# Ranking a recorded program's operations by the dependent chain behind them

## The chip, the cores and the metric

The kernel runs on one core of a Trainium2 chip. The metric is device time in microseconds of one launch, the median of several runs; lower is better. The core has TensorE (PE in the profile, with its weight loads as PEld), VectorE (DVE), ScalarE (ACT), GpSimd (POOL, unused here) and SyncE (SP), which issues the DMAs. Each engine works off its own instructions in the order in which the program holds them, and waits at an instruction until what it needs has been signalled.

## The reference

Two request groups, `p` with 1024 tokens and `s` with 512, go through the same two layers. In each layer

```python
hn = rmsnorm(h, norm_g[l])
z = hn @ w_in[l]                                  # 1024 -> 3328 columns
o_hg  = hgrn2_branch(...)     # gated linear recurrence, chunks of 64, both directions
o_lru = rglru_branch(...)     # width-4 convolution, two gates, linear scan, both directions
o_da  = diff_attn_branch(...) # difference of two softmaxes, 4 heads, partial rotary
o = jnp.concatenate([o_hg, o_lru, o_da], axis=-1)
h = h + o @ w_out[l]
gate = jax.nn.sigmoid(h @ ple_gate_w[l])
h = h + gate * (p[l] @ ple_w[l])
```

and a last rmsnorm follows. Everything is float32.

## The kernel before

**Tiles.** Activations lie transposed, 128 features by 512 tokens. A product with a weight is done in three passes on operands that are split into a rounded part and a remainder: weight hi times x hi, weight lo times x hi, weight hi times x lo. So every weight tile `wr` (128x512) is loaded by a DMA (L351), rounded by ACT into `wh` (L352), and its remainder `wl` is made by DVE (L353). `proj` (L356 on) issues, for each tile of four 128x128 blocks, three groups of four matmuls, one for each pass, all through the helper `mm` (L309), into a PSUM bank named `pj`.

**Stages.** For a layer and a group, stage A (`phase_a`) projects to queries, keys, values, gates and recurrence inputs, writes these to DRAM, and then runs three sessions that read them back: attention `at` (`attn`, scores into `big`, row maximum `nm` L664, exponential `pp` L667, difference L674, transposes L682, product with the values into `ov`), the LRU (`lru`, its own weight tile `gwr` L718, its gate matmuls into `big` L746, tanh and exponentials on ACT L753 to L757, products and scans on DVE L767 to L790) and HGRN2 `hg` (`hg_unit` with six levels of products on DVE and small 64x64 matmuls, then `hg_fin`). Attention and HGRN2 end in `head_tail`: a transpose into `pt` (L490), a norm on DVE, a second transpose (L506), a product with the gate. Stage B (`phase_b`) does the output product, the gate product and the residual, and sums squares for the next norm in `acc` (L1095), which `stats_rs` hands to PE (L376). The order of the stages is A of `p`, A of `s`, B of `p` (two blocks of 512 tokens), B of `s`, twice.

**What sets the order.** The code doesn't issue anything directly. Each call is recorded as an operation (`Recorder.__call__`) with its engine, an estimated occupation `occ` and latency `lat`, and the operations that it depends on. `order` then plays a list scheduler: time after time it takes, over all engines, the ready operation that could begin earliest, and on an engine, among those that could begin at once, the one with the lowest `prio`. Before, the priority is the number of the operation in the recording order plus offsets written by hand: weight tiles 400 earlier (`WOFF`), evictions of projections 900 earlier (`EVAC`), statistics 2000 earlier. Buffers of a role are handed out in recording order. `issue` then emits the instructions in that order, and this is the order in which each engine's queue holds them on the chip.

```python
o.prio = o.seq + self.off + off                   # L85
...
def push(o):
    bisect.insort(ready[o.eng], (o.prio, o.seq))  # L133
```

**Buffers that the steps below speak of.** There are two `big` accumulators (each two PSUM banks), three `pj` banks, four `wr` tiles shared by all weight loads, `gwr` among them, and two `ev` tiles for evictions on their way to DRAM.

Of the kernel before, what the change touches and what calls it, by code (L numbers as in the profile page):

```python
# [13 lines left out]
AF = mybir.ActivationFunctionType  # L14
# [18 lines left out]
        "m2x": 9, "m4x": 9, "m2y": 8, "m4y": 6}  # L33
WOFF, EVAC = 400, 900
BANKS = {"pj": 3, "pt": 2, "ov": 1}
LANE = {
# [6 lines left out]
class T:  # L43


    __slots__ = ("tag", "shape", "dt", "name", "t", "uses", "end", "role", "cls", "first")
# [12 lines left out]
class Op:  # L59
    __slots__ = ("eng", "occ", "lat", "fn", "deps", "succ", "nd", "rt", "new", "old", "prio", "seq", "fin", "tab", "nbytes", "stage", "c0", "c1")  # L60


class Recorder:
# [54 lines left out]
    def order(self):  # L118
# [3 lines left out]
        for o in ops:  # L122
            for d in o.deps:
                ops[d].succ.append(o.seq)
        free = {e: 0.0 for e in ("PE", "DVE", "ACT", "POOL", "SP")}
        ready = {e: [] for e in free}
# [111 lines left out]
def tile_trunk(ctx: ExitStack, tc: tile.TileContext, a, groups, depth):  # L238
    nc = tc.nc
# [41 lines left out]
    def V(w, fn, r, wr, ps_=0.0, sc=0.0, off=0):  # L281
        occ = 0.07 + w / 960.0 + ps_ + sc if w > 64 else 0.075
        return R("DVE", occ, fn, r, wr, lat=occ + (0.09 if w > 64 else 0.1), off=off)

    def A(w, fn, r, wr, extra=0.0, tab="exp", off=0):
        occ = 0.07 + w / 1200.0 + extra
        return R("ACT", occ, fn, r, wr, lat=occ + 0.11, tab=tab, off=off)

    def PE(occ, fn, r, wr, off=0):
        return R("PE", occ, fn, r, wr, lat=occ + 0.2, off=off)  # L290
# [13 lines left out]

    MM = 0.236
    B2 = 128 * 512 * 4
# [208 lines left out]
    def phase_a(l, g, n, xs, mid):  # L515
# [105 lines left out]
        def attn(hf):  # L621
# [16 lines left out]
            for tb in range(nb):  # L638
# [9 lines left out]
                for qt in range(4):  # L648
                    wts = []
                    for H in range(2):  # L650
                        P = []
                        s2 = small("s2", 1)
                        for j in range(2):
# [4 lines left out]
                            def f(pv=pv, k=k, q=q, qt=qt):  # L658
# [8 lines left out]
                            A(n, lambda p=p, pv=pv, nm=nm, s1=s1, s2=s2, j=j, qt=qt, H=H: nc.scalar.activation(  # L667
                                out=p.t, in_=pv(), func=AF.Exp, bias=nm.t, accum_out=s1[:, qt, H : H + 1] if j == 0 else s2.t), [b, nm], [p, sk], extra=0.28)
                            P.append(p)
# [17 lines left out]
                    for kb in range(nb):  # L687

                        def f(kb=kb, wts=wts, ov=ov, qt=qt):
                            for kt in range(4 * kb, 4 * kb + 4):  # L690
                                for H in range(2):
                                    mm(ov[H * 64 : H * 64 + 64, qt * 128 : qt * 128 + 128], dv[kt // 4][:, kt % 4, H * 64 : H * 64 + 64],
                                       wts[H][:, kt * 128 : kt * 128 + 128], start=kt == 0, stop=kt == n // 128 - 1)

                        PE(0.83, f, [dv[kb], (wts[0], kb), (wts[1], kb)], [ov])
                e2 = small("e2")
# [99 lines left out]
        def hg_unit(hp_, tb, ro, keep):  # L796
# [23 lines left out]
            def scores(kt, rk, rhs):  # L820
# [7 lines left out]

                PE(0.5, f, [kt, rk], [b])
                return b, lambda: b[:, :, 0:256].rearrange("p h (t i) -> p h t i", t=4)  # L830
# [6 lines left out]
            for li, bb in enumerate(LEVELS):  # L837
                yield
                nbk = 512 // bb
                kc = M2("kc")  # L840
                A(512, lambda kc=kc, bb=bb: nc.scalar.copy(kc.t.rearrange("p (x h r) -> p x h r", h=2, r=bb), diag(KP.t, bb)), X(KP), [kc], extra=0.06)  # L841
                b, pv = scores(kc, QP, lambda p, c, bb=bb: diag(QP[p], bb, c * 64, 64))
# [8 lines left out]

                ex = 0.15 if li % 2 == 0 else 0.0
                V(512, lambda bb=bb, tk=tk: nc.vector.tensor_tensor(out=diag(KP.t, bb), in0=diag(KP.t, bb), in1=tk(), op=MUL), [*X(KP), *tkeys], X(KP), sc=ex)  # L853
# [37 lines left out]

            PE(0.8, f, [*X(KT), v], [pi])
            E = M4("E")
# [10 lines left out]

            PE(0.5, f, [v, ST], [po])
            o2 = T("m2y", [128, 2, 4, 64], F32, "o2", ro.get("o2"))
# [349 lines left out]
```

## Time and profile before

| | |
|---|---|
| median of 3 runs | 2166.9 us (2164.67 to 2170.54) |
| the profiled execution: its own time | 2168.66 us |
| the profiled execution: span from first to last instruction | 2166.9 us |
| PE busy | 2033.9 us, 94% of the span |
| DVE busy | 1540.7 us, 71% |
| ACT busy | 1146.5 us, 53% |
| mean granted TensorE clock | 0.966 of full speed |
| DMA | 318.63 MB, mean 147 GB/s |

The page gives busy time as a share of the whole span, then the same in 40 slices, with the clock that the chip granted to TensorE in each slice. A group of instructions is told with its total and mean time, and the idle time of the engine just before it with what ended it. The table by windows gives each engine's busy time in a stretch that one chooses, and the timeline gives the instructions one by one, with what each waited for in brackets. TensorE's clock has two levels, 1.2 and 2.4 GHz; a granted clock of 0.91 over a stretch means that it stood at the lower one for 18% of it.

### The profile page before, as it was taken

How to read it: one execution, taken by the hardware profiler on the slowest of the kernel's cores; microseconds unless marked ns; L12 is line 12 of the kernel's file. 1: busy time of each engine (PE TensorE's matmuls, PEld its weight loads, DVE VectorE, ACT ScalarE, POOL GpSimd, SP SyncE). 2: the span in 40 equal slices, each digit the busy share in tenths (PEclk: the TensorE clock that was granted, in tenths of full speed). 3: DMA queues.
4: the chain of work that ended last, by engine and by line, in shares of the span. 5: the costliest groups of instructions: out<-in, count | busy, mean ns of one | idle time of the engine just before them, and what ended most of it. 6: DMA issues, size and time to landing. Idle time of an engine off the chain costs nothing.

```text
span 2166.9 us, 38237 instructions
## 1 busy us (share of the span) xinstructions
PE 2033.9 (94%) x14584; PEld 1663.2 (77%) x14584; DVE 1540.7 (71%) x2921; ACT 1146.5 (53%) x1957; POOL 0.2 (0%) x4
## 2 busy tenths in 40 slices
PE   7998999999999888999979988999999999989897
PEld 6887887788887676877758876778778878667786
DVE  5425867788898888754462658686999988874654
ACT  4215866667555337643332557666745654853332
POOL 0000000000000000000000000000000000000000
PEclk9999989999999999999989989999999999999998
DMA  4336423355353446565543453232464344646462
GB/s 149 112 110 195 143 97 116 105 159 167 127 159 113 146 155 198 174 217 162 175 156 117 128 170 121 83 120 90 126 203 157 123 155 161 202 148 220 133 217 73
DMA packets 187576, 318.63 MB, mean 147 GB/s; under 512 B 22017, under 2 KB 40961, under 8 KB 187393
## 3 DMA queue, kind: packets, MB, share of 16 engines
q1 hardware_dynamic: 187392, 316.19, 45.4%
q8 instruction: 115, 1.88, 0.4%
q14 instruction: 69, 0.56, 0.1%
HBM read 231.16 MB, written 84.93 MB: 146 GB/s over the span
## 4 chain that ended last, share of the span: by engine, by line
PE 65%; DVE 6%; ACT 5%; DMA 5%; issue 2%; SPq 0%; DVEq 0%; ACTq 0%
PE pj L309 48%; PE big L309 8%; PE ov L309 4%; PE pt L682 3%; PE pt L309 1%; DMA qk_p<-ev 1%; DMA p<-in_p_p 1%; DMA qk_s<-ev 1%; ACT tr L753 1%; DVE wl L353 1%; ACT tr L757 1%; ACT ti L753 1%; DMA cs<-in_c_cos 1%; PE pt L506 1%; ACT L761 0%
## 5 line engine op out<-in xcount | busy, mean ns | idle before, releaser
L309 PE MATMUL pj<-act,wh 128*128 128x512 f32 x3648 | 946.6, 399 | 22.9 <-ACT act L320 13.7
L309 PEld LDWEIGHTS pj<-act,wh 128*128 128x128 f32 x3648 | 684.1, 191 | 174.1 <-ACT act L320 18.0
L309 PE MATMUL pj<-act,wl 128*128 128x512 f32 x1824 | 489.1, 399 | 2.1 <-DVE wl L353 2.1
L353 DVE TENSOR_TENSOR wl<-wr,wh 128x512 fp32r<-128x512 f32 x400 | 271.6, 686 | 204.0 <-PE pj L309 145.2
L352 ACT CAST wh<-wr 128x512 fp32r<-128x512 f32 x400 | 244.3, 620 | 299.7 <-PE pj L309 228.9
L309 PEld LDWEIGHTS pj<-act,wl 128*128 128x128 f32 x1824 | 343.9, 192 | 76.4 <-DVE wl L353 3.0
L667 ACT ACTIVATE pp<-big,nm 128x1024 f32<-128x1024 f32 (+1 forms) x192 | 187.4, 977 | 72.9 <-DVE nm L664 67.0
L664 DVE TENSOR_REDUCE nm<-big 128x1 f32<-128x1024 f32 (+1 forms) x192 | 198.0, 1034 | 14.9 <-PE big L309 14.3
L309 PE MATMUL pj<-wh,act 128*128 128x256 f32 x768 | 148.8, 292 | 2.7 <-DVE ev L321 2.7
L309 PEld LDWEIGHTS pj<-wh,act 128*128 128x128 f32 x768 | 127.0, 197 | 9.8 <-DVE ev L321 3.3
L685 ACT COPY wt<-pt 128x512 f32<-128x512 f32 x160 | 93.0, 587 | 64.0 <-PE pt L682 56.0
L309 PE MATMUL big<-ks,qs 96*128 96x512 f32 x320 | 113.4, 428 | 9.3 <-ACT pp L667 8.5
L309 PE MATMUL pj<-wl,act 128*128 128x256 f32 x384 | 110.8, 288 | 0.9 <-DVE wl L353 0.8
L674 DVE SCALAR_TENSOR_TENSOR pp<-pp,cc 128x1024 f32<-128x1024 f32 (+1 forms) x96 | 105.6, 1100 | 0.8
L682 PE MATMUL pt<-ident,pp 128*128 128x128 f32 x640 | 94.6, 277 | 3.7 <-ACT ev L612 2.8
L682 PEld LDWEIGHTS pt<-ident,pp 128*128 128x128 f32 x640 | 75.5, 141 | 22.0 <-ACT ev L612 3.2
L309 PE MATMUL ov<-wt,dv 128*64 128x128 f32 x1280 | 88.2, 279 | 0.4 <-ACT wt L685 0.4
L309 PEld LDWEIGHTS ov<-wt,dv 128*64 128x64 f32 x1280 | 68.6, 136 | 22.0 <-issue 18.4
L309 PEld LDWEIGHTS pj<-wl,act 128*128 128x128 f32 x384 | 75.3, 196 | 1.5 <-DVE wl L353 1.5
L309 PE MATMUL pj<-act,ph 128*128 128x512 f32 x192 | 62.7, 403 | 14.3 <-ACT act L320 10.6
L309 PEld LDWEIGHTS big<-ks,qs 96*128 96x128 f32 x320 | 55.2, 192 | 22.6 <-ACT pp L667 11.3
L841 ACT COPY kc<-KP 128x512 f32<-128x512 f32 x72 | 48.5, 674 | 42.9 <-DVE KP L853 32.6
(186 smaller groups left out, 2467.7 us busy)
## 6 DMA issues: line engine op xcount, KB each, us to landing
wr<-in_w_in SPq DMA_DIRECT2D x176, 256.0 KB
wr<-in_w_out SPq DMA_DIRECT2D x96, 256.0 KB
wr<-in_w_gate SPq DMA_DIRECT2D x96, 256.0 KB
h_p<-bh SPq DMA_DIRECT2D x48, 256.0 KB
sg_p<-ev SPq DMA_DIRECT2D x32, 256.0 KB
wr<-in_w_v SPq DMA_DIRECT2D x32, 256.0 KB
qk_p<-ev SPq DMA_DIRECT2D x32, 256.0 KB
act<-oT_p SPq DMA_DIRECT2D x32, 256.0 KB
```

Of the source, the lines that this page charges most:

```text
L309: nc.tensor.matmul(out, lhsT, rhs, start=start, stop=stop, skip_group_check=True)
L352: A(w, lambda raw=raw, hi=hi: nc.scalar.copy(hi.t, raw.t), [raw], [hi], off=o)
L353: V(w, lambda raw=raw, hi=hi, lo=lo: nc.vector.tensor_tensor(out=lo.t, in0=raw.t, in1=hi.t.bitcast(F32), op=SUB), [raw, hi], [lo], off=o)
L506: PE(0.436, lambda: [nc.tensor.transpose(pb[:, c], ot[:, c], ident) for c in cols], [ot, "ident"], [pb])
L664: V(n, lambda nm=nm, pv=pv: nc.vector.tensor_reduce(out=nm.t, in_=pv(), axis=mybir.AxisListType.X, op=ALU.max, negate=True), [b], [nm])
L667: A(n, lambda p=p, pv=pv, nm=nm, s1=s1, s2=s2, j=j, qt=qt, H=H: nc.scalar.activation(out=p.t, in_=pv(), func=AF.Exp, bias=nm.t, accum_out= ...
L674: V(n, lambda P=P, c=c: nc.vector.scalar_tensor_tensor(out=P[0].t, in0=P[1].t, scalar=c.t, in1=P[0].t, op0=MUL, op1=ADD), [P[0], P[1], c], ...
L682: nc.tensor.transpose(pt[:, kt * 128 : kt * 128 + 128], P[0][:, c0 : c0 + 128], ident)
L685: A(512, lambda wt=wt, pt=pt, kb=kb: nc.scalar.copy(wt[:, blk(kb)], pt.t), [pt], [(wt, kb)])
L753: A(512, lambda dst=dst, pg=pg, gt=gt, dr=dr, hb=hb, col=col: nc.scalar.activation(out=dst[:, dr, :], in_=pg[:, gt, :], func=AF.Tanh, scal ...
L757: A(512, lambda tr=tr, dr=dr, col=col: nc.scalar.activation(out=tr[:, dr, :], in_=tr[:, dr, :], func=AF.Exp, scale=d["n4"][:, col], bias=d ...
L841: A(512, lambda kc=kc, bb=bb: nc.scalar.copy(kc.t.rearrange("p (x h r) -> p x h r", h=2, r=bb), diag(KP.t, bb)), X(KP), [kc], extra=0.06)
```

## The change

Each operation gets a `rank`: its own estimated latency plus the largest rank among those that depend on it, so the estimated length of the longest dependent chain that starts with it. The rank in microseconds, times `RANK` (1.0), is taken off the priority. The offsets written by hand stay. Beside that, estimated durations are changed: matmuls, the fixed parts of DVE and ACT operations, and single operations of attention and HGRN2. No operation is added, removed or given other operands; what is issued differs in its order alone.

```diff
+RANK = 1.0
...
+        for o in reversed(ops):
+            o.rank = o.lat + max((ops[x].rank for x in o.succ), default=0.0)
+        for o in ops:
+            o.prio -= o.rank * RANK
         free = {e: 0.0 for e in ("PE", "DVE", "ACT", "POOL", "SP")}
...
     def V(w, fn, r, wr, ps_=0.0, sc=0.0, off=0):
         occ = 0.07 + w / 960.0 + ps_ + sc if w > 64 else 0.075
-        return R("DVE", occ, fn, r, wr, lat=occ + (0.09 if w > 64 else 0.1), off=off)
+        return R("DVE", occ, fn, r, wr, lat=occ + (0.06 if w > 64 else 0.08), off=off)
 
     def A(w, fn, r, wr, extra=0.0, tab="exp", off=0):
-        occ = 0.07 + w / 1200.0 + extra
-        return R("ACT", occ, fn, r, wr, lat=occ + 0.11, tab=tab, off=off)
+        occ = 0.085 + w / 1200.0 + extra
+        return R("ACT", occ, fn, r, wr, lat=occ + 0.08, tab=tab, off=off)
...
-    MM = 0.236
+    MM = 0.2305
...
-                                out=p.t, in_=pv(), func=AF.Exp, bias=nm.t, accum_out=s1[:, qt, H : H + 1] if j == 0 else s2.t), [b, nm], [p, sk], extra=0.28)
+                                out=p.t, in_=pv(), func=AF.Exp, bias=nm.t, accum_out=s1[:, qt, H : H + 1] if j == 0 else s2.t), [b, nm], [p, sk], extra=0.18)
...
-                        PE(0.83, f, [dv[kb], (wts[0], kb), (wts[1], kb)], [ov])
+                        PE(0.98, f, [dv[kb], (wts[0], kb), (wts[1], kb)], [ov])
...
-                PE(0.5, f, [kt, rk], [b])
+                PE(0.3, f, [kt, rk], [b])
...
-                ex = 0.15 if li % 2 == 0 else 0.0
+                ex = 0.0
...
-            PE(0.8, f, [*X(KT), v], [pi])
+            PE(0.55, f, [*X(KT), v], [pi])
...
-            PE(0.5, f, [v, ST], [po])
+            PE(0.35, f, [v, ST], [po])
```

One more estimate of the same kind, that of the copy `kc`, goes from 0.06 to 0.2 extra. The new lines push the code down by five lines, so that what is L309 before is L314 after, L506 is L511, and so on.

**PE at the end of layer 0's sessions.** `o` and `ot` are the tiles of `head_tail`, `pj` the projections, `big<-q,kc` the first matmuls of HGRN2 of group `s`. Before:

```order
L309 MATMUL pj<-act,wl 128x512 x4
L309 MATMUL pj<-act,wh 128x512 x4
L309 MATMUL ov<-wt,dv 64x128 x8
L490 MATMUL pt<-ident,o 128x128 x4
L506 MATMUL pt<-ident,ot 128x128 x4
L309 MATMUL pt<-QP,E 64x64 x30
L490 MATMUL pt<-ident,o 128x128 x4
L506 MATMUL pt<-ident,ot 128x128 x8
L309 MATMUL pj<-act,wh 128x512 x8
L309 MATMUL pj<-act,wl 128x512 x8
```

And with the change:

```order
L314 MATMUL pj<-act,wh 128x512 x4
L511 MATMUL pt<-ident,ot 128x128 x4
L314 MATMUL ov<-wt,dv 64x128 x8
L314 MATMUL pj<-act,wh 128x512 x4
L314 MATMUL pj<-act,wl 128x512 x4
L495 MATMUL pt<-ident,o 128x128 x4
L314 MATMUL pj<-act,wh 128x512 x12
L314 MATMUL big<-q,kc 64x64 x16
L314 MATMUL pj<-act,wl 128x512 x4
L314 MATMUL big<-QP,kc 64x64 x16
L314 MATMUL pj<-act,wl 128x512 x4
L314 MATMUL pj<-act,wh 128x512 x4
```

Before, the three last transposes of `ot` follow each other with no projection between them, and only stage B's first projections come behind. Now the last but one of them stands second in the piece, projections of stage A stand between all of them, the last of them comes six rows below the piece, and the first matmuls of the next HGRN2 unit have moved up among the projections.

**SP in stage A of layer 1, group `p`.** `gwr` is the weight tile of the LRU's second quarter, `qk_p` the evicted queries and keys on their way to DRAM, `nh` the next group's input. Before:

```order
L789 DMA sg<-sg_p 128x512
L589 DMA qk_p<-ev 8x16x512
L351 DMA wr<-in_w_in 128x512
L589 DMA qk_p<-ev 8x16x512
L476 DMA nh<-h_s 128x512
L351 DMA wr<-in_w_in 128x512
L476 DMA nh<-h_s 128x512
L589 DMA qk_p<-ev 8x16x512 x2
L476 DMA nh<-h_s 128x512
L589 DMA qk_p<-ev 8x16x512 x2
L718 DMA gwr<-in_lru_w 128x512
```

And with the change:

```order
L794 DMA sg<-sg_p 128x512
L723 DMA gwr<-in_lru_w 128x512
L594 DMA qk_p<-ev 8x16x512
L735 DMA zp<-lx_p 128x514
L594 DMA qk_p<-ev 8x16x512
L796 DMA oT_p<-s 128x512
L481 DMA nh<-h_s 128x512
L356 DMA wr<-in_w_in 128x512 x2
```

The load of `gwr` has moved past six writes of `qk_p`, two weight loads and three loads of `nh`. On PE the four groups of gate matmuls that need it have moved up by 12 groups.

**DVE at the end of stage B of layer 1, group `p`, first block.** `acc` is the sum of squares that PE waits for, `ti` and `T` are LRU tiles of group `s`. Before:

```order
L353 TENSOR_TENSOR wl<-wr,wh 128x512
L770 SCALAR_TENSOR_TENSOR T_20347<-tr,T_20347 128x1024
L771 TENSOR_TENSOR ti<-ti,T_20347 128x1024
L1095 TENSOR_TENSOR acc<-acc,ev 128x512
L1086 SCALAR_TENSOR_TENSOR ev<-ev,pj 128x512
L775 SCALAR_TENSOR_TENSOR ti<-tr,ti 128x512
L1087 SCALAR_TENSOR_TENSOR h_19819<-ev,h_19819 128x512
L783 SCALAR_TENSOR_TENSOR ti<-tr,ti 128x512
L1095 TENSOR_TENSOR acc<-acc,ev 128x512
```

And with the change:

```order
L1092 SCALAR_TENSOR_TENSOR h_19791<-ev,h_19791 128x512
L772 SCALAR_TENSOR_TENSOR ti<-ti,u 128x1024
L330 TENSOR_TENSOR act<-act 128x512
L1100 TENSOR_TENSOR acc<-acc,ev 128x512
L330 TENSOR_TENSOR act<-act 128x512
L336 TENSOR_SCALAR rv<-ov 128x4
L775 SCALAR_TENSOR_TENSOR T_20381<-tr,T_20381 128x1024
L339 TENSOR_SCALAR ry<-rv 128x4
L776 TENSOR_TENSOR ti<-ti,T_20381 128x1024
```

Two products and two scans of the LRU, which stood ahead of the last addition to `acc`, now stand behind it.

## Rows read from the trace of the kernel before

**Rows 1.** The page: span, busy time, and granted clock in 40 slices.

```profile
span 2166.9 us, 38237 instructions
...
PE 2033.9 (94%) x14584; PEld 1663.2 (77%) x14584; DVE 1540.7 (71%) x2921; ACT 1146.5 (53%) x1957; POOL 0.2 (0%) x4
...
PEclk9999989999999999999989989999999999999998
```

**Rows 2.** Windows: stretch, length, PE, PEld, DVE, ACT, POOL busy; PEclk, DMA.

```profile
702.00:756.00 54.00, 45.75 (x582) 35.78 (x580) 45.78 (x108) 21.27 (x36) 0.00 (x0) 0.91 0.43 138
756.00:810.00 54.00, 48.27 (x563) 38.42 (x556) 44.31 (x110) 21.37 (x36) 0.00 (x0) 0.91 0.48 162
1737.00:1791.00 54.00, 54.00 (x616) 42.58 (x614) 45.70 (x108) 25.79 (x48) 0.00 (x0) 1.00 0.48 160
1791.00:1845.00 54.00, 54.00 (x632) 43.69 (x632) 47.91 (x115) 24.11 (x41) 0.00 (x0) 1.00 0.49 162
1242.00:1296.00 54.00, 44.53 (x255) 38.89 (x254) 27.26 (x37) 28.97 (x42) 0.00 (x0) 0.87 0.62 181
1296.00:1350.00 54.00, 45.79 (x248) 37.63 (x246) 46.60 (x63) 40.53 (x61) 0.00 (x0) 0.91 0.41 131
1890.00:1944.00 54.00, 46.00 (x192) 37.11 (x193) 39.43 (x67) 33.07 (x52) 0.00 (x0) 0.91 0.36 119
```

**Rows 3.** Waits of PE: who for whom, us in total, times, longest us.

```profile
PE ov L309 <- DVE acc L1095: 18.7, 4, 7.9
...
PE big L309 <- ACT pp L667: 8.5, 4, 6.7
PE pt L506 <- DVE ot L502: 6.8, 3, 4.3
PE big L309 <- ACT gwh L320: 6.7, 2, 4.0
...
PE big L309 <- DVE ul L321: 5.6, 2, 3.0
...
PE pj L309 <- DVE wl L353: 2.9, 5, 1.4
```

**Rows 4.** Timeline from 702 us: start, length, engine, instruction, idle before it.

```profile
718.35 1.09 PE L506 MATMUL pt<-ident,ot 128*128 128x128 f32 x4 [4.29 <-DVE ot L502]
...
719.09 3.76 PE L309 MATMUL pj<-act,wh 128*128 128x512 f32 x8
```

**Rows 5.** Timeline from 1239 us, stage A of layer 1, group p.

```profile
1239.93 1.98 PE L309 MATMUL pj<-act,wh 128*128 128x512 f32 x8
...
1242.97 0.33 SPq L351 DMA_DIRECT2D wr<-in_w_in  x1
...
1258.76 0.40 SPq L718 DMA_DIRECT2D gwr<-in_lru_w  x1
...
1263.83 0.62 ACT L320 CAST gwh<-gwr 128x512 fp32r<-128x512 f32 x1 [2.45 <-DMA gwr<-in_lru_w]
...
1264.50 0.79 PE L309 MATMUL big<-uh,gwh 128*128 128x512 f32 x1 [3.98 <-ACT gwh L320]
```

**Rows 6.** Timeline from 1326 us, attention of layer 1, group p.

```profile
1333.41 1.20 DVE L664 TENSOR_REDUCE nm<-big 128x1 f32<-128x1024 f32 x1
...
1335.90 1.22 PE L309 MATMUL big<-ks,qs 96*128 96x512 f32 x2 [6.72 <-ACT pp L667]
```

**Rows 7.** Timeline from 1921 us, end of stage B's first block, layer 1.

```profile
1921.55 1.23 DVE L770 SCALAR_TENSOR_TENSOR T<-tr,T 128x1024 f32<-128x1024 f32 x1 [1.83 <-ACT T L761]
...
1928.72 1.87 PE L309 MATMUL ov<-ones,acc 128*128 128x1 f32 x8 [7.92 <-DVE acc L1095]
```

**Rows 8.** Windows of the densest stretch: all engines, then DVE on `wl` alone.

```profile
432.00:702.00 270.00, 268.12 (x2932) 218.15 (x2927) 240.25 (x508) 164.81 (x315) 0.00 (x0) 1.00 0.46 144
...
432.00:702.00 270.00, 36.54 (x54) 1.00 0.46 144
```

More of the change, by code (lines that the diff above doesn't have):

```diff
@@ L59 @@
 class Op:
-    __slots__ = ("eng", "occ", "lat", "fn", "deps", "succ", "nd", "rt", "new", "old", "prio", "seq", "fin", "tab", "nbytes", "stage", "c0", "c1")
+    __slots__ = ("eng", "occ", "lat", "fn", "deps", "succ", "nd", "rt", "new", "old", "prio", "seq", "fin", "tab", "nbytes", "rank", "stage", "c0", "c1")
 class Recorder:
@@ L840, in hg_unit @@
                 kc = M2("kc")
-                A(512, lambda kc=kc, bb=bb: nc.scalar.copy(kc.t.rearrange("p (x h r) -> p x h r", h=2, r=bb), diag(KP.t, bb)), X(KP), [kc], extra=0.06)
+                A(512, lambda kc=kc, bb=bb: nc.scalar.copy(kc.t.rearrange("p (x h r) -> p x h r", h=2, r=bb), diag(KP.t, bb)), X(KP), [kc], extra=0.2)
                 b, pv = scores(kc, QP, lambda p, c, bb=bb: diag(QP[p], bb, c * 64, 64))
```

## The prediction

> **What bounds the kernel now.** I read the page first, then the granted clock, then the windows, then the waits of PE, and last the timeline around the longest of these waits. On the page PE is busy 2033.9 of 2166.9 us [rows 1]: TensorE is the bound, and 133 us of its span are idle. No other engine comes near; DVE has 1540.7. So the order of the work is worth what PE's idle time and its slow clock cost, and no more than that. The row of the clock says where: most slices stand at nine tenths or more, and the eights are few [rows 1]. The windows show such places beside one that is free of them [rows 2]. The clock costs twice: where PE has idled, the next matmuls run at the lower of the two levels. Eight matmuls take 3.76 us at 719.09 [rows 4], just after a wait, and 1.98 in undisturbed work [rows 5].
>
> The profiled execution took 2168.66 us, 1.8 us more than its span and 1.8 more than the median of the runs (2166.9). I sum against 2168.66 and take the 1.8 off at the end.
>
> **The change part by part.** The estimated durations and the rank cost nothing on the chip: they are used while the program is recorded, and the same instructions are issued with the same operands. ACT's table loads, which an order could multiply, are 49 in both. So everything lies in what stands in front of what. Between the places below the order changes too, in nearly all of the A stages; stage B keeps PE's order over long pieces, and with it the waits for `acc` at its block ends, which are 18.7 us in four waits [rows 3]. Three of these I leave as they are, at 10.8 us.
>
> *End of layer 0's sessions (702 to 810 us).* Here the projections of group `s` have run out before the chains of attention and HGRN2 are through. The two last transposes of `ot` wait for DVE's norm with nothing between them; the longer wait is 4.29 us [rows 4], and the line L506 loses 6.8 in all [rows 3]. In the changed order projections of stage A stand between these transposes, and HGRN2 of `s` starts among them, so the wait is covered by work that has to be done anyway. The trace has a picture of it: layer 1 does the same work at 1737 to 1845 us, and there the order of before already has this interleaving. PE is busy 54.00 and 54.00 of 54 us at a clock of 1.00 there, and in layer 0 45.75 and 48.27 at 0.91 [rows 2]. The bounds: by matmuls, layer 0 gets 582 + 563 = 1145 done in 108 us and layer 1 616 + 632 = 1248, so at layer 1's rate 1145 would take 99.1, a gain of 8.9. By time, 8.25 + 5.73 = 14.0 us of idle time, and a clock of 0.91 is 19.4 us at the lower level over both windows together, in which at most 9.7 are lost, some of them idle anyway; with half of that the gain is 18.9. Rates differ with the mix of matmuls, so I take the middle of the lower part: **12**, with 8.9 and 18.9 as ends. What is late next if the cover holds: nothing in layer 1's picture.
>
> *Start of the LRU's second quarter in layer 1 (1242 to 1296 us).* PE is busy 44.53 of 54 us [rows 2]: 9.5 idle. The evictions of rope hold the two `ev` tiles until their DMA has landed, PE's banks aren't freed, and the gate matmuls that could fill in come only after `gwr`, issued at 1258.76 behind those same evictions in SP's queue and cast at 1263.83; PE stood 3.98 us for it [rows 5]. The change takes `gwr` past six eviction writes, three loads of `nh` and two weight loads; what it delays by that is one issue of 0.33 to 0.40 us [rows 5], and the weight load that had the buffer before it. It needs a free `wr` tile, and the next one was free at 1242.97, when a weight took it [rows 5]. From issue to cast took 5.07 us, from cast to PE's start 0.67 [rows 5]: PE could begin at 1242.97 + 5.07 + 0.67 = 1248.7. But its gate groups moved up by twelve as well: two groups take the eight matmuls of 1.98 us at 1239.93 [rows 5], and two more behind them bring PE there at about 1243.6. So a wait of some 5.1 us takes the place of 9.5: 4.4 gained. Of the clock, 0.87 over 54 us is 14 us at the lower level, at most 7.0 lost; a wait of 5 us will cost some of that again, so I add 1.6. I take **6**, ends 0 and 16.5 (9.5 + 7.0).
>
> The Trainium skill's page "DMA: Bandwidth & Descriptors", section "Anatomy of one DMA — SWDGE (gpsimd) path", gives a fit for one transfer, measured on GpSimd's path: 2.0 us plus the bytes over 436 GB/s. For these 256 KB that is an estimate of 2.6 us; the trace has 5.07 for it, on SP's path. By the page PE would wait 2.5 us less and the gain would be 8.5; the trace is taken.
>
> *Attention of layer 1, group `p` (1296 to 1350 us).* One score waits 6.72 us for a `big` accumulator, because the row maximum that has to read it starts on DVE only at 1333.41, behind LRU products and scans [rows 6]; the stretch has 8.2 us idle and a clock of 0.91 [rows 2]. In the changed order nineteen groups of matmuls (eleven of the value projection, four sets of transposes, four of LRU gates) stand between this score and the one before, where three stood. They would have to last 0.35 us each to cover 6.72, and a group of four matmuls lasts 0.9 [rows 5]. Four of them are transposes that hang on the same DVE queue, so about 2 us of waiting may come back there. I take **6**, ends 0 and 13.1 (8.2 and at most 4.9 for the clock).
>
> *Last `acc` of layer 1's first block (1921 to 1929 us).* PE waits 7.92 us [rows 7]. Two products and two scans of the LRU, each 1.23 us or close to it [rows 7], move from ahead of the last addition to behind it: 4.9 us off that queue. ACT still has its LRU functions ahead of the square that feeds it, so I take **3**, ends 0 and 7.9.
>
> *First gates of the LRU elsewhere.* The waits for `gwh` and `ul` are 6.7 + 5.6 = 12.3 us in four [rows 3]; without the 3.98 counted above 8.3 are left. `gwr` is issued earlier there too, but PE also comes earlier. I take **3**, ends 0 and 8.3.
>
> Sum of the gains: 12 + 6 + 6 + 3 + 3 = 30. Against it stand waits at places that the reshuffle makes new. Before, no row shows them; the nearest are the waits of PE in group 3, from none to one like the longest there, 7.9 [rows 3]. I take two of 3 us, so **-6**; below it is nothing, above it all 30. The sum is 2168.7 - 24 = 2144.7, less 1.8: **2143 us**.
>
> **The rivals.**
>
> *Everything closes.* All five ends together are 18.9 + 16.5 + 13.1 + 7.9 + 8.3 = 64.7, and no new wait: 2168.7 - 64.7 - 1.8 = 2102. For it: layer 1 has 108 us without a gap [rows 2], so such orders exist. Against it: `gwr` can't land before PE asks for it.
>
> *No change.* The stalls move and add up to the same: 2167, within 6 us (0.3%), which is about what a measurement of this kernel can tell from no change. For it: the rank acts among neighbours, since the offsets of 400, 900 and 2000 stay; a wait that is closed in one place was often a buffer that is late in the next. This is also the case in which the change doesn't do what it says, because the scheduler takes whatever is ready first, and ranks only decide among what is ready together.
>
> *Weight remainders come late.* A weight tile's `wl` opens a short chain: once the projection is done, an eviction. LRU, attention and HGRN2 have long ones, so the rank puts their DVE work ahead of `wl` where they are ready together. DVE is a strict queue in its order as the timeline shows it: the row maximum of group 6 stood behind products that nobody waited for. The stretch 432 to 702 us has DVE at 240.25 of 270 us and 54 remainders of 36.54 us in all [rows 8], 0.68 each. If PE comes to stand half a remainder, 0.34 us, for each of these and for as many in the same stretch of layer 1, that is 37 us, and the end is 2168.7 - 24 + 37 - 1.8 = 2180, slower than before. It decides from the point at which PE's wait for `wl`, 2.9 us now [rows 3], passes 24. For it: 30 us of spare time in 270 on DVE isn't much. Against it: PE idles only 1.9 us in that stretch [rows 8], and `wl` keeps its offset of 400.
>
> **How the numbers follow.** The forecast, with its terms between their ends, gets 0.58 and covers 2110 to 2160. The case in which everything closes gets 0.10, no change 0.15, late remainders and other new waits 0.17. Faster by over 0.3% (under 2160) is 0.58 + 0.10 = 0.68, the same 0.15, slower by over 0.3% (over 2173) 0.17. The range leaves out most of the best case, some 0.08, and the worse part of the slower one, 0.12: 2110 to 2172.
>
> **What would show it.** Right: in the windows at 702 to 810 us PE is busy 105 us or more of 108 at a clock near 1.00; the wait of L506 (now L511) falls under 2 us; `gwr` in layer 1 is issued about 15 us ahead of where it was, and PE's wait for it is about 5 us while the others around it are gone; the longest wait of a score for `pp` falls under 2.5; the wait for `acc` loses about 3 of 18.7. Wrong: PE's total idle time stays near 133 us; or PE's wait for `wl` rises from 2.9 to over 24 us; or DVE in the dense stretch leaves PE under 260 of 270 us.

## The result, and the profile after

The changed kernel takes 2142.86 us (median of 4 runs, 2131.24 to 2143.37), the kernel before beside it 2167.18. The ratio is 0.9874, with a 95% interval from 0.9838 to 0.991. Measured once more on another chip, later, it is 0.9887 (0.986 to 0.9914). So the change is faster by 1.1 to 1.3%, and 2143 was forecast. How these 24 us came about is another matter: some terms of the sum were far off, and the errors cancelled.

The profiled execution took 2142.88 us. The page of the changed kernel:

```profile
span 2140.9 us, 38230 instructions
...
PE 2032.1 (95%) x14584; PEld 1658.7 (77%) x14584; DVE 1534.6 (72%) x2921; ACT 1149.3 (54%) x1957; POOL 0.2 (0%) x4
...
PEclk9999989999999999999989989999999999999998
```

PE does the same matmuls in nearly the same busy time. What went is idle time: 2140.9 - 2032.1 = 108.8 us instead of 133 [rows 1]. The mean granted clock rose from 0.966 to 0.969. With 1 as the upper level and 0.5 as the lower, that is 2 x 0.031 x 2140.9 = 133 us at the lower level instead of 2 x 0.034 x 2166.9 = 147.

The windows answer to [rows 2]; the first two of layer 1 stand 13 us earlier, about as far as the kernel had come ahead there, and the third 10 us earlier, where it was 22 ahead. The last is the dense stretch of [rows 8].

```profile
702.00:756.00 54.00, 54.00 (x837) 42.07 (x832) 48.57 (x102) 22.03 (x37) 0.00 (x0) 1.00 0.39 123
756.00:810.00 54.00, 46.30 (x265) 36.11 (x257) 42.51 (x100) 32.79 (x52) 0.00 (x0) 0.94 0.62 202
1229.00:1283.00 54.00, 44.04 (x251) 38.24 (x252) 29.77 (x40) 31.31 (x44) 0.00 (x0) 0.84 0.66 199
1283.00:1337.00 54.00, 53.06 (x308) 45.51 (x309) 47.37 (x60) 50.00 (x73) 0.00 (x0) 1.00 0.34 113
1880.00:1934.00 54.00, 46.95 (x195) 37.47 (x195) 43.77 (x73) 33.57 (x52) 0.00 (x0) 0.91 0.53 171
432.00:702.00 270.00, 267.88 (x2998) 217.63 (x2994) 238.89 (x533) 164.06 (x311) 0.00 (x0) 1.00 0.47 148
```

The first window is full and at full clock, the second is not. The window of the LRU's start (1229) is as idle as before, but it holds more work: the last 4.6 us of its idle time stand ahead of gate matmuls that came at 1300 us before, outside the window. The attention behind it (1283) is nearly full. The dense stretch lost nothing.

The waits of PE in the changed kernel, in the columns of [rows 3] (code lines there are 5 further down):

```profile
PE pj L314 <- ACT act L325: 27.4, 16, 6.6
PE ov L314 <- DVE acc L1100: 15.1, 4, 4.4
...
PE big L314 <- DVE ul L326: 8.9, 4, 4.6
...
PE big L314 <- ACT gwh L325: 2.3, 1, 2.3
PE big L314 <- DVE gwl L326: 2.2, 1, 2.2
PE big L314 <- ACT pp L672: 2.2, 4, 1.0
...
PE pj L314 <- DVE wl L358: 0.2, 1, 0.2
```

The wait of L506, now L511, has no row any more. The wait for `pp` fell from 8.5 to 2.2, that for `acc` from 18.7 to 15.1, and that for `wl` didn't rise. The top row, projections that wait for a hi split on ScalarE, was there before with nearly the same sum:

```profile
PE pj L309 <- ACT act L320: 24.4, 21, 2.6
```

New in it are two long waits, of 6.2 and 6.6 us, where the longest was 2.6.

**Where the lead comes from.** Both kernels issue the same TensorE operations, and at many points both have issued exactly the same set of them. At each such point the start of the next TensorE operation in the two traces gives the lead of the changed kernel:

| before, us | 232 | 817 | 1119 | 1230 | 1244 | 1281 | 1305 | 1408 | 1856 | 1858 | 1932 | 2046 | end |
|---|---|---|---|---|---|---|---|---|---|---|---|---|---|
| lead, us | 3.9 | 1.4 | 14.9 | 15.8 | 13.3 | 21.4 | 15.0 | 30.0 | 28.8 | 22.8 | 22.2 | 24.5 | 25.9 |

Between 232 and 817 us the sets differ. There I weigh each kind of matmul group by what it takes undisturbed (the tenth percentile of start to start in the trace before) and compare when both had done equal work, which is rougher. By that the lead is 3.3 us at 232, -6.3 at 270, -8.7 at 700, 10.7 at 790, 1.4 at 817. Other weights (every matmul by itself, or PE's busy time times the granted clock) give 9 to 18 us for the loss up to 700, 18 to 24 for the gain from there to 790 and 7 for the loss behind it. Leads are from one profiled execution each, and the one of the kernel before is among its slower ones, so that a lead at the end can stand some us above the gain in medians (6.8 against 3.2 for TensorE's order alone, below); the second trace of the change gives 16.1 at 1119, 22.3 at 1281 and 27.4 at the end. So the end of layer 0's sessions gave about 19 us, some 12 had been lost ahead of it, most of that by 270 us, and about 9 were lost right behind it. The loss by 270 has these windows; first the kernel before, then the changed one:

```profile
216.00:270.00 54.00, 52.22 (x291) 45.18 (x290) 47.23 (x62) 48.45 (x72) 0.00 (x0) 0.97 0.42 144
```

```profile
216.00:270.00 54.00, 50.19 (x238) 41.96 (x237) 46.22 (x63) 41.95 (x63) 0.00 (x0) 0.89 0.46 143
```

PE waits there for `ev` and comes to the lower clock earlier. For the loss at 790 the timeline of the changed kernel shows ScalarE and PE, and the same at 1829:

```profile
795.48 1.28 ACT L766 ACT_TABLE_LOAD   x1
796.78 1.06 ACT L766 ACTIVATE T<-T 128x1024 f32<-128x1024 f32 x1
...
798.25 1.13 ACT L325 CAST act<-p 128x512 fp32r<-128x512 f32 x2
...
798.91 1.31 PE L314 MATMUL pj<-act,ph 128*128 128x512 f32 x2 [6.20 <-ACT act L325]
800.02 1.91 PE L314 MATMUL pj<-act,wh 128*128 128x512 f32 x4
...
1835.58 1.32 PE L314 MATMUL pj<-act,ph 128*128 128x512 f32 x2 [6.58 <-ACT act L325]
```

The two `p` tiles of the first output block are split behind the LRU's functions and their table load in ScalarE's queue. PE, which has come early, stands for them, and then runs at the lower clock: four matmuls take 1.91 us, where 1.07 is usual in both kernels.

### The profile page after: what moved, and what is told of

Read it like the earlier page. It is cut to its first block, busy times and chain, and to the rows that moved or that the text cites. A ratio compares the mean times of both kernels' runs of the same rounds, so it can differ in the third digit from the quotient of the medians.

```text
span 2140.9 us, 38230 instructions
## 1 busy us (share of the span) xinstructions
PE 2032.1 (95%) x14584; PEld 1658.7 (77%) x14584; DVE 1534.6 (72%) x2921; ACT 1149.3 (54%) x1957; POOL 0.2 (0%) x4
## 4 chain that ended last, share of the span: by engine, by line
PE 77%; DMA 7%; DVE 7%; ACT 6%; issue 2%; SPq 1%; DVEq 0%; ACTq 0%
PE pj L314 57%; PE big L314 9%; PE ov L314 6%; PE pt L687 3%; DMA qk_p<-ev 2%; PE pt L314 2%; DVE wl L358 1%; ACT L766 1%; ACT tr L758 1%; DMA ks<-qk_p 1%; ACT T L766 1%; ACT tr L762 1%; PE pt L495 0%; DMA oT_p<-s 0%; PE pt L511 0%
## 5 line engine op out<-in xcount | busy, mean ns | idle before, releaser
L314 PE MATMUL pj<-act,wh 128*128 128x512 f32 x3648 | 952.4, 399 | 15.1 <-ACT act L325 8.1
L314 PEld LDWEIGHTS pj<-act,wh 128*128 128x128 f32 x3648 | 683.2, 190 | 165.3 <-ACT act L325 11.4
L314 PE MATMUL pj<-act,wl 128*128 128x512 f32 x1824 | 495.3, 399 | 0.2 <-DVE wl L358 0.2
L314 PEld LDWEIGHTS pj<-act,wl 128*128 128x128 f32 x1824 | 344.1, 192 | 75.9 <-DVE wl L358 1.5
L314 PE MATMUL pj<-wh,act 128*128 128x256 f32 x768 | 148.0, 291 | 0.0
L314 PEld LDWEIGHTS pj<-wh,act 128*128 128x128 f32 x768 | 126.1, 196 | 6.3 <-issue 0.5
L314 PE MATMUL big<-ks,qs 96*128 96x512 f32 x320 | 114.6, 431 | 3.1 <-ACT pp L672 2.0
L314 PE MATMUL pj<-wl,act 128*128 128x256 f32 x384 | 110.2, 287 | 0.0
L546 DVE SCALAR_TENSOR_TENSOR ev<-ev,pj 128x512 f32<-128x512 f32 x60 | 40.8, 683 | 69.4 <-ACT ev L545 69.4
L314 PE MATMUL ov<-wt,dv 128*64 128x128 f32 x1280 | 88.3, 279 | 0.4 <-ACT wt L690 0.4
L314 PEld LDWEIGHTS ov<-wt,dv 128*64 128x64 f32 x1280 | 68.6, 136 | 22.7 <-issue 19.4
L314 PE MATMUL pj<-act,ph 128*128 128x512 f32 x192 | 64.0, 410 | 22.4 <-ACT act L325 19.3
L545 ACT ACTIVATE ev<-pj 128x512 f32<-128x512 f32 x60 | 35.7, 599 | 73.7 <-PE pj L314 70.5
L314 PEld LDWEIGHTS pj<-wl,act 128*128 128x128 f32 x384 | 75.2, 196 | 0.0
```

What stands on the lines that cost most here:

```text
L314: nc.tensor.matmul(out, lhsT, rhs, start=start, stop=stop, skip_group_check=True)
L545: A(512, lambda: nc.scalar.activation(out=s.t, in_=p.t, func=AF.Tanh, scale=0.5), [p], [s])
L546: V(512, lambda: nc.vector.scalar_tensor_tensor(out=s.t, in0=s.t, scalar=1.0, in1=p.t, op0=ADD, op1=MUL), [s, p], [s])
```

## The experiments

My theory: the rank makes the gain, by putting short TensorE products and the operations that feed them ahead, so that projections are left to fill the ends. The rivals: the re-measured durations make it; any reshuffling of this size would. All experiments start from the kernel before with its old durations unless said otherwise. They ran on several chips; each ratio is to the kernel before on the same chip.

### The rank alone

```diff
+RANK = 1.0
...
+        for o in reversed(ops):
+            o.rank = o.lat + max((ops[x].rank for x in o.succ), default=0.0)
+        for o in ops:
+            o.prio -= o.rank * RANK
```

> The planner's order with the chain length subtracted from every priority (RANK = 1), and all durations as before. If the chain length makes the gain (theory): 2141 to 2152 us, three quarters or more of the 24 us, with the 4.3 us wait of L506 and the long waits of the score for pp gone. If the re-measured durations make it (rival 1): 2163 to 2171. If any reshuffling would do as well (rival 2): anywhere from 2135 to 2190, and then the order without the chain length and the shaken order must spread as widely.

2127.9 us, ratio 0.9853 (0.9827 to 0.9879). The rank alone gives all of the gain. It gives more than I expected: with that ratio a kernel of 2167 us would take 2135, which is under the range of 2141 to 2152. Its windows and waits:

```profile
702.00:756.00 54.00, 54.00 (x675) 42.35 (x674) 51.13 (x107) 23.91 (x41) 0.00 (x0) 1.00 0.50 167
756.00:810.00 54.00, 52.77 (x484) 42.80 (x483) 45.42 (x109) 30.33 (x52) 0.00 (x0) 1.00 0.63 208
```

```profile
PE pj L314 <- ACT act L325: 14.3, 12, 2.2
PE big L314 <- DVE ul L326: 12.0, 5, 6.2
PE ov L314 <- DVE acc L1100: 10.7, 3, 3.6
PE big L314 <- ACT gwh L325: 10.7, 2, 7.5
```

The ends of the sessions are closed further than in the change (106.8 of 108 us against 100.3), and the long waits for the `p` splits are not there: the longest on that row is 2.2. The LRU's gates, on the other hand, wait longer than in the change, up to 7.5 us for `gwh` and 6.2 for `ul`. Its lead is 19.9 us at 833, 24.1 at 1119, 30.1 at 1288, 22.3 at 1305 and 33.9 at the end.

### The durations alone

```diff
-    MM = 0.236
+    MM = 0.2305
...
-                        PE(0.83, f, [dv[kb], (wts[0], kb), (wts[1], kb)], [ov])
+                        PE(0.98, f, [dv[kb], (wts[0], kb), (wts[1], kb)], [ov])
```

and seven more of the change's durations.

> Nine of the ten re-measured durations (the latency of VectorE's operations stays as before, since with all ten and no chain length the planner comes to a state in which nothing can be issued), and no chain length. Theory: 2158 to 2174 us, within 0.4% of before, because the order between two operations that are both ready is still the order in which they were written. Rival 1 (durations): 2138 to 2150.

2148.38 us, ratio 0.9941 (0.9922 to 0.9961). The time lies in the range of the rival (2138 to 2150), but that was set against 2167 for the kernel before, which took 2162.3 on this chip; with the ratio it would be 2154, between the two. So neither theory had it: the durations are worth 0.6% by themselves, most of it in layer 0 (lead 13.1 us at 1119 and 17.4 at the end). Which of the nine does it stays open.

### A shaken order

```diff
+        for o in ops:
+            o.prio += (o.seq * 7919 % 1009 / 1009 - 0.5) * JIT
```

with JIT = 60.

> The planner of before with its old durations, where every priority gets a fixed number between -30 and +30 that has nothing to do with the chains behind it (a spread of 17, as wide as that of the chain lengths about their trend, 18). Theory: no gain, 2165 to 2195 us, because an order that ignores the chains moves as many waits onto TensorE as away from it. Rival 2 (any reshuffle): below 2160 is as likely as above.

2172.85 us, ratio 1.0056 (1.0035 to 1.0077): slower. The end of layer 0's sessions got worse in its first window and better in its second (before: 45.75 and 48.27 us). A wait says where (line 506 of before is 509 here):

```profile
702.00:756.00 54.00, 39.83 (x466) 32.20 (x466) 35.06 (x91) 14.39 (x25) 0.00 (x0) 0.84 0.31 105
756.00:810.00 54.00, 53.86 (x755) 42.62 (x755) 48.70 (x106) 27.60 (x48) 0.00 (x0) 1.00 0.54 182
```

```profile
PE pt L509 <- DVE ot L505: 10.2, 3, 5.2
```

The lead is -14.3 us at 709 and -2.5 at 838, so most of this came back at once. What the order loses for good lies in layer 1: the lead is 8.0 at 1336 and -6.4 at 1940.

### The rank with its sign turned

```diff
+            o.prio -= o.rank * RANK
```

with RANK = -1.

> Old durations; the chain length is added to the priority's number and no longer subtracted, so that the operation with the shortest chain behind it goes first. It moves as much as the chain length does (TensorE operations by 10.4 places on average, 9.5 with the right sign). Theory (the sign matters): slower than before, 2175 to 2200 us. Rival (any reshuffle of that size gains): below 2160.

2176.27 us, ratio 1.0062 (1.0036 to 1.0088): slower, at the low end of what was expected. The transposes of `ot` wait longer than before (12.1 us against 6.8), and one hi split, of an activation, costs 9.4 us at once:

```profile
PE pj L314 <- ACT act L329: 18.3, 6, 9.4
...
PE pt L511 <- DVE ot L507: 12.1, 5, 5.3
```

Here too most of the loss is in layer 1, where the 9.4 us stand at 1936: the lead is -1.5 at 1119 and -11.4 at 1943. Two orders that ignore or turn the chains are slower, the one that follows them is faster. That any reshuffle would do is out, as far as two of them can show it; that an order without the rank can gain by luck is not, since the durations alone gave 0.6%.

### One layer at a time

Against the rank alone:

```diff
-            o.prio -= o.rank * RANK
+            o.prio -= o.rank * RANK * (o.seq < 4323)
```

for layer 0, and the same with >= for layer 1.

> Old durations; the chain length counts for the operations of layer 0 only, so that layer 1 keeps its written order. The order with the chain length everywhere stood 24.1 us ahead of the kernel before at the last cut at which both have done the same TensorE work in layer 0 (1119 us), and 33.9 at the end. Theory (each layer's ends of sessions are shortened where they stand): a gain of 16 to 24 us, most of it between 690 and 810 us. Rival (chance: a reshuffled order gains or loses 10 us anywhere): the gain of layer 0 may come out as anything from -5 to 25, and this run and the one of layer 1 do not add up to the 34.

> Old durations; the chain length counts for the operations of layer 1 only. Theory: a gain of 6 to 14 us, none of it before 1110 us, most of it at the LRU's and attention's start (1240 to 1340 us). Rival (chance): anything from -10 to 15, and no sum with the run of layer 0.

Layer 0: 2141.66 us, 0.9894 (0.9863 to 0.9925). Layer 1: 2157.83 us, 0.996 (0.9942 to 0.9978). The gains of 1.06 and 0.40% add up to 1.46, and the rank on both gave 1.47; the intervals of the two would allow a sum from 1.1 to 1.8. So far the two layers are separate gains, as the theory says, and about seven tenths lie in layer 0. The lead of the first is 17.6 us at 833, 22.3 at 1119 and 25.4 at the end, so its layer 1 is as before but for 3 us. That of the second is -0.6 us at 1119, -0.9 at 1305, 6.6 at 1858 and 5.9 at the end. Of the expected places in layer 1, the LRU's start gave 6.7 us by 1288 and lost them by 1305, as in the change, and the attention behind it made the gain: by equal work the lead is 14.1 at 1408, more than half of which is lost again.

### TensorE's order alone, and the other queues alone

Against the rank alone:

```diff
-            o.prio -= o.rank * RANK
+            o.prio -= o.rank * RANK * (o.eng == "PE")
```

and the same with != for ScalarE, VectorE and SP.

> Old durations; the chain length counts only where two operations of TensorE are compared; VectorE, ScalarE and the transfers keep their written order. Theory as the prediction had it (TensorE does the LRU's and the heads' short products early and has projections left to fill the ends): most of the gain, 2135 to 2150 us. Rival: the gain comes from the queues of ScalarE, VectorE and SP, which feed TensorE; then this is 2155 to 2175.

> The other half: the chain length counts on ScalarE, VectorE and SP only, and TensorE keeps its written order. Theory: 2150 to 2170 us. Rival (the feeding queues make the gain): 2128 to 2145.

TensorE alone: 2161.39 us, 0.9994 (0.9973 to 1.0015), no gain. The others alone: 2154.96 us, 0.9956 (0.9941 to 0.9971). Together the halves give 0.5%, the whole 1.5%. The theory fell in the form in which I had it, and so did the rival. The windows at the end of the sessions, TensorE alone first, then the others:

```profile
702.00:756.00 54.00, 50.31 (x645) 38.78 (x645) 49.29 (x110) 22.20 (x36) 0.00 (x0) 1.00 0.53 169
756.00:810.00 54.00, 49.53 (x520) 40.51 (x516) 45.31 (x110) 29.98 (x48) 0.00 (x0) 0.97 0.57 184
```

```profile
702.00:756.00 54.00, 51.32 (x646) 40.70 (x643) 47.56 (x115) 22.98 (x41) 0.00 (x0) 0.97 0.50 163
756.00:810.00 54.00, 48.47 (x536) 38.69 (x534) 45.10 (x110) 22.53 (x40) 0.00 (x0) 0.94 0.49 162
```

Here the halves do add: PE is busy 94.0 us of 108 before [rows 2], 99.8 with either half and 106.8 with both. What is missing comes later. With the others alone the lead hardly grows any more, from 8.4 us at 1119 to 9.6 at the end. With TensorE alone it is 14.9 us at 1119 but 6.8 at the end, and its rows of waits, from which this is the part that grew, show why:

```profile
PE pj L314 <- ACT act L325: 26.7, 18, 8.3
PE ov L314 <- DVE acc L1100: 19.7, 4, 8.9
PE big L314 <- ACT pp L672: 10.3, 10, 4.4
```

PE comes early to a split or a sum that ScalarE and VectorE still have in the old place. With the others alone the same two waits are 6.6 and 8.3 us at their longest. In this kernel the rank is worth its 1.5% only where the order on all engines follows it.

### The new stalls, taken away

From the changed kernel. The two pairs of splits are moved in the finished order, and nothing else:

```diff
+            if g == g0 and tb == 0:
+                R.early.append(len(R.ops) - 2)
...
+        for c in self.early:
+            i = out.index(self.ops[c])
+            cast, sub = out.pop(i), self.ops[c + 1]
+            out.remove(sub)
+            left = 8
+            while left:
+                i -= 1
+                left -= out[i].eng == "ACT"
+            out[i:i] = [cast, sub]
```

> The changed kernel's order, with two pairs of operations moved and nothing else: the hi and lo splits of the two p tiles of the first output block in each layer stand 8 ScalarE operations earlier, ahead of the LRU's functions and of their table load. Theory: the two new waits of TensorE at those splits (6.20 and 6.58 us) fall under 1 us each, and the half-clock stretch behind them shrinks: 2126 to 2133 us, 10 to 17 below the change. Rival: the waits only move to the next late thing (the p tiles' transfers, or the LRU's functions that now come 1.1 us later): 2138 to 2145.

2142.68 us, ratio 0.9911 (0.989 to 0.9932), no better than the change (0.9874 and 0.9887). The rival is right, in a way I hadn't seen. PE and ScalarE at both places:

```profile
792.62 0.89 PE L325 MATMUL pj<-act,ph 128*128 128x512 f32 x2
...
806.14 0.41 ACT L368 CAST ph<-pr 128x256 fp32r<-128x256 f32 x1
...
806.60 1.22 PE L325 MATMUL pj<-act,ph 128*128 128x512 f32 x2 [6.71 <-ACT ph L368]
...
1842.21 0.62 ACT L336 CAST uh<-u 128x512 fp32r<-128x512 f32 x1 [5.18 <-DVE u L752]
...
1846.12 1.22 PE L325 MATMUL pj<-act,ph 128*128 128x512 f32 x2 [10.27 <-ACT ph L368]
```

Both old waits are gone: PE goes on at 792.62 without one. But it then stands 6.71 and 10.27 us for the next split, of the weight `ph`, which is queued behind the same LRU work and behind splits and evictions of the output block. At the first place ScalarE is busy 16.51 of the 16.57 us from 789.98 to 806.55, so the sum of its work is the limit; at the second it stands 5.18 us in its queue for the LRU's `u`. The total idle time of PE is as it was: 2140.8 - 2030.4 = 110.4 us.

### The change itself, once more

> The changed kernel itself once more, beside the order with chain lengths and old durations (which was measured in another call, 0.9853 of before, against 0.9874 for the change). If the re-measured durations add their 0.6% to the chain length's 1.5%: a ratio near 0.980. If they add nothing once the chain length sets the order: 0.985 to 0.989. If they take something back: above 0.989.

2137.47 us, ratio 0.9887 (0.986 to 0.9914). The rank's 0.9853 and the durations' 0.9941 would multiply to 0.9795, which is outside the interval: the two gains don't add. Against the rank alone, the durations may take a little back or do nothing. The intervals overlap, so which it is stays open. The run of the durations had nine of the ten, so the tenth, the latency of VectorE's operations, may have a part in it as well. The row by which the change is behind the rank alone is the one with the `p` splits, here as in the first trace of the change:

```profile
PE pj L314 <- ACT act L325: 26.8, 14, 6.6
```

### Two ways to more

The first counts a transfer in a chain with 2.8 us more, against the rank alone:

```diff
-            o.rank = o.lat + max((ops[x].rank for x in o.succ), default=0.0)
+            o.rank = o.lat + (2.8 if o.nbytes else 0.0) + max((ops[x].rank for x in o.succ), default=0.0)
```

> Old durations and chain lengths, where a transfer counts in a chain with 2.8 us more, about what the planner itself adds to it (0.6 + 0.94 + 1.8 us, less its issue); in the change a transfer counts with its issue alone, 0.47 us. Theory (late transfers at the starts of stretches, such as the gate weights of the LRU that TensorE awaited for 7.49 us, are what the chain length misses): 2115 to 2128 us, and that wait under 3 us. Rival (chance, as the planner's greedy choice moves everything behind it): 2125 to 2150.

2140.66 us, ratio 0.9907 (0.9881 to 0.9933). The theory fell: its aim, the wait for the gate weights, is longer, with the load issued at 1214.62:

```profile
1214.62 0.40 SPq L723 DMA_DIRECT2D gwr<-in_lru_w  x1
...
1222.29 0.80 PE L314 MATMUL big<-uh,gwh 128*128 128x512 f32 x1 [8.35 <-ACT gwh L325]
```

The order now does reach this place earlier than any other, with a lead of 31.6 us at 1244 by equal work, and PE asks for the weights earlier by as much. In layer 1 it then lost to a `p` split (6.6 us) and to `acc` (6.6).

The second way is RANK = 2 with the old durations.

> Old durations, RANK = 2.0. If the weight of the chain length were a dose: 2105 to 2125 us. If once is enough to order what is near (the chain lengths spread by 18 about their trend, two neighbouring steps of a session stand some tens of numbers apart): 2125 to 2145, no better than with RANK = 1 (0.9853).

2145.36 us, ratio 0.9921 (0.9896 to 0.9946): less than with 1 (0.9853). The weight is no dose, as far as one other value shows it.

No version beats the change for certain. The rank with the old durations has the lowest ratio, 0.9853, and its interval overlaps that of the change. Over all runs, the five orders with the rank on every engine and in both layers lie between 0.9853 and 0.9921, and the three that ignore it or turn its sign between 0.9941 and 1.0062. So that the rank gains is shown; which of two ranked orders is the better by half a percent may be chance.

## Why the prediction was right, and where it was wrong

The total was right (2143 against 2142.86) and so was the cause: PE's idle time, much of it at session ends, closed by the order of ready operations, with the durations behind it at no cost of their own. That the total agrees so closely is luck, since gains and losses were both about 30 us larger than forecast. Term by term, from the leads:

- *End of layer 0's sessions*, 12 forecast, ends 8.9 and 18.9. By equal work about 19 were gained from 700 to 790, at the upper end or past it. The mechanism was right: the first window is full at a clock of 1.00, and the wait of L506 is gone. But the sign that I gave, 105 of 108 us, failed with 54.00 + 46.30 = 100.3, as the new wait of 6.20 us falls in it. The step that failed is the sentence that nothing would be late next: I read it off layer 1, where the output block didn't come as early.
- *Start of the LRU's second quarter*, 6 forecast. The size was right, but it didn't last. The lead is 15.8 at 1230, ahead of the first of these waits, and 21.4 at 1281, where both kernels have issued the gates of this quarter: 5.7 us (5.4 in the second trace of the change). `gwr` came 32 us earlier, not 15, but about 16 of these are the lead that the kernel had by then: 1226.73 and 15.8 are 1242.5, and 1242.97 was forecast for the free `wr` tile. PE then waited 2.28 us for `gwr` instead of 5.1, and two short waits followed:

```profile
1226.73 0.33 SPq L723 DMA_DIRECT2D gwr<-in_lru_w  x1
...
1230.21 0.52 PE L314 MATMUL big<-uh,gwh 128*128 128x512 f32 x1 [2.28 <-ACT gwh L325]
1233.37 0.79 PE L314 MATMUL big<-uh,gwl 128*128 128x512 f32 x1 [2.21 <-DVE gwl L326]
1237.40 0.79 PE L314 MATMUL big<-uh,gwh 128*128 128x512 f32 x1 [1.97 <-ACT tr L758]
...
1277.53 0.79 PE L314 MATMUL big<-ul,gwh 128*128 128x512 f32 x1 [4.58 <-DVE ul L326]
```

  The step that failed stands behind the term: no new wait was counted in the third quarter, whose gates come earlier as well. There PE stands 4.58 us for `ul`, and at 1305 the lead is back at 15.0. VectorE makes `ul` behind a product whose `sg` tile lands late:

```profile
1275.99 0.69 DVE L795 SCALAR_TENSOR_TENSOR s<-s,sg 128x512 f32<-128x512 f32 x1 [5.41 <-DMA sg<-sg_p]
1276.79 0.69 DVE L326 TENSOR_TENSOR ul<-u,uh 128x512 fp32r<-128x512 f32 x1
```

  From issue to cast the load of `gwr` took 2.82 us this time (the cast begins at 1229.55), where I had taken 5.07 from [rows 5]; with the rank alone it took 6.07 (1221.94 to 1228.01), so one row is no price for a load. The Trainium skill's fit of 2.0 us plus the bytes over 436 GB/s (page "DMA: Bandwidth & Descriptors", section "Anatomy of one DMA — SWDGE (gpsimd) path"), an estimate of 2.6 us here, is near the lowest of the three. The 2.5 us of gain that hung on it didn't come all the same, since the low half `gwl` and the accumulators were late behind it.
- *Attention of layer 1*, 6 forecast, upper end 13.1. The lead rose from 15.0 to 30.0 up to 1408. The window is nearly full (53.06 of 54 us) at 1.00, and the longest wait for `pp` is 1.0. Some 10 to 12 of the 15 came by 1350, by equal work. I had kept 2 us of waiting in it and half of the clock, and had not looked past 1350, where the kernel before is idle for another 5.4 us up to 1404.
- *Last `acc`*, 3 forecast: the longest wait fell from 7.92 to 4.40, so 3.5. A new wait of 1.9 us for a hi split follows right behind, and the lead is 21.4 at 1905 and 22.5 at 1930.
- *First gates elsewhere*, 3 forecast, ends 0 and 8.3: the lead is 3.9 at 232, but 1.3 of that stands from the first matmul on, so 2.6. The third of these waits stood in layer 0's first output block:

```profile
867.00 0.59 PE L309 MATMUL big<-ul,gwh 128*128 128x512 f32 x1 [2.65 <-DVE ul L321]
```

  It is gone, and from 848 to 893 the lead grew by 5.9 us, with the clock there at 1.00 instead of 0.92. A wait of 1.3 us for `pl` in that stretch went too, so the 5.9 are not this term's alone.
- *New waits*, -6 forecast, ends 0 and -30. This is the worst sized term. The two `p` splits cost about 9 us (790 to 817) and 6.0 (1856 to 1858), the wait for `ul` 6.4 (1281 to 1305), the start of attention in layer 0 some 12, which is about 34 together and past the end that I gave. The nearest row, the hi splits with 24.4 us in waits of up to 2.6, was not among [rows 3]. I named no place for the new waits, though one could be found in the order: in layer 0 the splits had moved behind a table load. In layer 1 they stood behind one before, too (the load at 1852.52, the first split at 1857.13), and PE hardly waited for them (0.5 and 0.8 us).
- *Not forecast at all*: the rest of the 13.5 us between 817 and 1119, some 7.6, in layer 0's output blocks. Waits for hi splits and for `ph` got shorter there at several places.

So 30 of gains and 6 of losses were, between the points above, some 62 and 36. The rival of late weight remainders did not come: the wait for `wl` went from 2.9 to 0.2 us (with the rank alone to 7.1, far from the 24 at which it would decide), and the dense stretch keeps 267.88 of 270 us. "No change" and "everything closes" had the right pieces in them, the one that stalls move, the other that full windows exist.

The experiments add what the trace before couldn't show: that the rank, and not the durations, carries it; and that TensorE's own order, on which I had rested the first term, closes about half of that place (99.8 us, between 94.0 and 106.8) and gives nothing in total without the other queues'.

## What to carry to other kernels

In this list-scheduled kernel the length of the dependent chain was a good second key beside the written order, at weight 1 and on all engines together; given to TensorE's queue alone it made that engine arrive early at waits for the others. Judge a new order by the lead at points of equal work, not by its total: here more than half of what was gained was lost again, nearly all of it at four places. And before moving one late operation ahead, look at what else stands behind the same work in that queue, because here the wait went to the next one.

## What the runs showed of the hardware

One program doesn't run at one speed. On the chip of the last runs the kernel before took 2152.42 to 2171.24 us in 12 executions, the same instructions in the same order, and its mean granted clock went along: 0.970 to 0.973 in the six below 2160 us, 0.965 to 0.969 in the six above. A difference of 0.5% between two orders therefore needs several executions of each: the rank alone took from 2122.76 us at a clock of 0.980 to 2134.79 at 0.975.
